# A transformer block in three-term fp32r products: fp32 products put next to each other on TensorE, and two queues reordered in the last rows

## The chip, the core and the metric

The kernel runs on one core of a Trainium2 chip. A core has a matrix engine (TensorE, PE in the profile, whose weight loads are listed as PEld), VectorE (DVE), ScalarE (ACT), GpSimd (POOL) and SyncE (SP), each with an instruction queue of its own that it works off strictly in order, and 16 DMA engines. Matmuls accumulate in PSUM, which here is used as eight banks of 128 x 512 fp32; the other tiles lie in SBUF.

The metric is the time of one execution on the chip, in microseconds (us), as the median of several runs. The profile is taken in an execution of its own, with its own time, and its span is a little shorter than that time.

## The reference, cut to what matters

One transformer block on 512 tokens of 1024 features: a gated linear attention (GLA, 4 heads, keys of 128, values of 256, forward and backward in time), a softmax attention with low-rank queries and keys (MLA, 8 heads, 96 features a head), both merged into one output projection, an MLP with a squared ReLU, and a final norm.

```python
def gla_direction(q, k, v, log_a, include_diag):
    ...
    scores = jnp.where(mask, jnp.einsum('bhnck,bhnsk->bhncs', q_dec, k_dec), 0.0)
    o_intra = jnp.einsum('bhncs,bhnsv->bhncv', scores, v)
    ...
def mla_branch(cq, ckv, kr, positions, g_q, w_uq, g_kv, w_ukv):
    ...
        s = jnp.einsum('bhqd,bhkd->bhqk', qblk, kt).astype(jnp.float32)
        p = jax.nn.softmax(s, axis=-1)
        return jnp.einsum('bhqk,bhkv->bhqv', p.astype(vt.dtype), vt)
    ...
def reference(...):
    h = x
    n = rmsnorm(h, g_mix[l])
    proj = n @ w_in[l]
    ...
    y_gla = gla_branch(...)
    y_mla = mla_branch(...)
    merged = jax.nn.sigmoid(z_ma) * y_gla + jax.nn.sigmoid(z_mb) * y_mla
    h = h + merged @ w_out[l]
    m = rmsnorm(h, g_mlp[l])
    h = h + jnp.square(jax.nn.relu(m @ w_ff1[l])) @ w_ff2[l]
    return rmsnorm(h, g_final)
```

## The kernel before

**Two kinds of products.** Results are wanted to fp32 accuracy. Most products are made of fp32r operands: each operand is split into a high part (an ACT copy to fp32r) and a low part (a DVE subtraction), and `mm3` (line 128) issues three matmuls, high by high, high by low, low by high, into one PSUM bank. Some products have plain fp32 operands instead: the transposes, which are matmuls with an identity matrix (`tp`, `y1`, `kt`, `mb`); the products of blocks `bd` and part of `sc` in the linear attention; and the sums over features by a column of ones (`ckvss`). The profile writes "f32" for both kinds; an fp32 product that is not a transpose stands in it as two records. A transpose is written as one. PSUM tiles come from `ps(tag, name)` (line 118) with two tags, "at" and "mm", of four banks each.

**Stages.** After projections of the input (to about 174 us in the trace), heads 0 to 2 of the linear attention run, each beside gates, projections and norms of the next (loop at `for h in range(GH - 1)`, instructions recorded as line 90). Then comes a stretch from head 3 of the linear attention through the whole softmax attention and the output projection (about 251 to 410 us, recorded as line 76), then the MLP in eight phases (line 90), and the last rows (about 704 us to the end, line 76).

**Orders written out by hand.** For the two stretches recorded as line 76, the class `Held` (line 58) first collects each instruction under its engine and the name of the tile that it writes, and `emit` then issues them in the order of a string, `SEQUENCE` or `LAST_ROWS`. An entry is an engine's letter (P TensorE, A ACT, D DVE, G GpSimd, S SyncE), the tile's name and a count: `P:tp000*4` is four matmuls into tile tp000. Since each engine works in order and waits by semaphores for the others, only the order within one engine counts; how the engines' entries interleave in the string does not. Outside these stretches the order of TensorE, ACT, DVE and GpSimd in the part in question is the program's order.

**Linear attention scores.** For a head, `gla_scores` (line 700) makes, with blocks of 128 tokens j = 0 to 3 of keys: `bd`, four products of the backward direction's diagonal blocks; `sc0` and `sc1`, one bank for two blocks of keys each, with the diagonal block and the neighbouring one; `kt`, four transposes of the keys for the state. From head 1 on, the even blocks of keys (j = 0, 2) are taken as a pair: `split_pairs` has split the keys and queries, and one `mm3` of 256 columns replaces two fp32 products. The odd blocks (j = 1, 3) stay two fp32 products each. Then ACT copies bd to SBUF (`bds`), and DVE's `copy_predicated` writes the part above the diagonal of bds into sc, for j = 0, 1, 2, 3 in turn; ACT rounds sc0 and sc1 to fp32r, DVE makes their low parts, and kt is split into `kT`. Head 0 has no pairs. For head 3 the same instructions stand in SEQUENCE.

Behind gla_scores, for heads 0 to 2, the program goes on with the next head's gates (`gatef` and `gateb`, then logarithms, scans and exponentials on ACT and DVE), a latent projection (`ckv` in head 2), the state, and so on. Head 2 ends with the products `ckv1`, `zb4`; zb4's weights are split on ACT (`zb4h`) and DVE (`zb4l`).

**Softmax attention.** For head h and 128 queries qt, `att_scores` makes a bank `s{h}{qt}` (three matmuls), DVE's maximum (`top`), ACT's exponential (`e`, with its sum `tot`); `att_normalise` scales e. `att_flip(h, half)` transposes two such e: bank `tp{h}{half}{g}`, g = 0, 1, four transposes each, and its split into `pT{h}{x}{g}`, ACT high, DVE low. `att_values` multiplies with the values (`av`). Beside these run the projections of two heads each, `uq`, `uk`, `uv`, and the first products of w_out (`wox`, `woz`, `wow`). `y1` (entries y14, y15) are the transposed outputs of the linear attention, `ckvss` the sums of squares of the latent, whose use DVE continues with `ckvr`.

**Last rows.** The output is finished row block by row block, 0 to 3, in `last_rows` (line 1878). For a block i, `h` is its sum with the MLP's output, `junk` the squares whose sums give the norm (into `hp`), and `ms` the output before it is stored: scaled by the gain and the norm. Row block 3's left half comes in two quarters; its last quarter is accumulated in bank `gend`, with which TensorE ends. `g341l` is the low part of a weight block for the last products.

Of the kernel before, what the change touches and what calls it, by code (L numbers as in the profile page):

```python
# [97 lines left out]
def tile_block(ctx: ExitStack, tc: tile.TileContext, t, out: bass.AP):  # L98
# [1922 lines left out]
    for x in range(2):  # L2021
# [3 lines left out]
        S:w2_11 S:zb6f S:w2_01 S:wr0f*2 A:sin A:zb6h D:cqc2 S:wk0f D:zb6l S:wr0f P:bd*4 D:cqc0 S:wr1f P:sc0*5  # L2025
        A:cqhl0 S:wr1f P:ckvss*4 D:ckvr D:cqc1 P:kt*4 S:wr1f D:ckvr P:y15*4 A:cqhl1 G:ckvr A:bds P:sc1*5 A:cqhl2
        D:sc0 P:y14*4 D:zb4 A:wr0h A:wk0h D:ckvr D:cqhl2 G:wr0l A:wk0h A:qF D:sc1*2 D:cqhl0 A:sc1 S:wk1f D:ckvrh
        D:ckvdg D:krsin D:ckvrl D:ckvdg D:cqhl1 D:sc1 P:zb5*24 A:wr1h D:sc0 A:yg4 D:zb5 G:wr1l A:cos D:kswap A:yg5
        G:wk0l S:wq0f P:ro0*9 A:kT D:kr P:ckvrs*2 S:wq0f A:wk1h A:wk0h G:wk1l S:wq0f A:sc0 D:roa1 G:qF A:wk0h
# [8 lines left out]
        S:q111 P:s11*3 A:yg6 G:wk2l D:tot00 D:e01 S:kbuf3 A:e00 G:wk1l D:top11 A:e03 S:q111 P:uk1*6 D:q101 S:bo11f
        A:kbuf2 P:s02*3 A:wq2h S:q111 A:e11 P:s10*3 G:wq2l S:bo11f D:top10 P:tp000*4 S:w2_20 D:top02 A:e10 A:e02
        P:uv11*12 P:tp001*3 A:wk2h D:tot02 D:kbuf2 A:pT000 G:wk2l D:tot10 A:tb6 S:kbuf3 D:pT010 P:uv10*12 P:tp001  # L2040
        S:w2_00 A:v10 P:s12*3 A:e02 S:q100 D:top12 A:pT001 S:q100 D:e03 A:bo11h S:wk3f D:v10 P:uv00*12 S:q101 A:yg7
        P:s13*3 P:uq2 D:top13 A:v00 S:kbuf2 P:tp010*4 A:e10 D:e11 S:q101 D:pT011 A:e13 D:v00 A:e12 P:uq2*8 D:bo11l
        A:wk2h A:pT000 P:s31*3 G:wk2l A:tb7 P:tp011*4 D:top31 S:wq3f A:wk3h P:tp100*4 P:av0 D:pT010 A:q200 S:wq3f
        A:e31 D:q201 D:tot12 P:uk2*6 D:e13 A:kbuf0 P:tp101*4 S:q301 A:pT001 P:s21*3 S:h3 A:wk2h D:pT011 A:e12
        G:wk2l D:top21 A:pT101 S:bo10f A:pT100 D:pT111 S:bo10f A:e21 P:av0*11 D:pT110 S:wq3f A:wk3h P:tp110*4
        D:kbuf0 A:pT100 P:s20*3 A:v11 D:pT110 S:kbuf1 P:s23*3 S:w2_00 D:top23 P:s22*3 S:q211 D:tb0 A:e23 P:tp111*4
        S:q210 D:top20 G:my0 A:pT101 S:q210 D:top22 A:e20 G:mx0 P:uv20*12 S:w2_10 D:pT111 A:bo10h P:s33*3 D:tot20
        D:top33 A:e22 P:s30*3 D:e21 S:q201 A:e33 P:s32*3 D:top32 S:q200 D:tot22 D:top30 A:e32 S:q200 D:bo10l A:e20
        S:kbuf0 A:e22 S:q201 P:av1*12 D:e23 A:e30 S:bo20f P:tp201*4 A:pT201 D:tot30 P:tp200*4 D:tb1 S:q300 A:pT200
        P:tp210*4 D:pT211 G:mx0 A:wk3h P:s53*3 A:e30 D:tot32 D:pT210 G:my0 A:pT200 D:top53 G:w2_00 D:pT210  # L2050
        P:uv21*12 A:wq3h P:tp211*4 D:e31 A:e53 P:s52*3 P:av2 A:pT201 D:top52 A:gao0 P:s43*3 D:top43 A:e52 G:gao0
        P:s40*3 D:pT211 A:v20 D:top40 A:e43 P:av2*5 G:wk3l D:tot52 D:v11 G:wq3l A:e40 P:tp300*4 D:e33 P:s42*3 A:e32
        G:wk3l S:bo21f A:e52 D:e53 P:s41*3 P:uq3 S:w2_30 G:wk3l P:tp301*4 D:top41 S:q310 A:pT301 D:v20 S:bo21f
        A:e41 P:av2*5 D:top42 S:w2_01 A:v21 S:q311 A:pT300 D:v21 S:w2_21 D:pT310 P:uq3*8 S:w2_11 A:q300 D:tot40
        P:s51*3 P:av2 A:e42 S:q300 D:top51 P:tp310*4 S:q301 D:tb2 A:pT300 S:w2_31 A:e51 D:tot42 D:pT310 P:uk3*6
        S:q311 A:e40 D:e43 S:w2_21 P:s50*3 D:e41 A:q310 G:my1 D:pT311 S:q310 P:tp311*4 A:pT301 P:tp401*4 D:top50
        G:mx1 S:bo20f A:e42 D:pT311 S:w2_31 A:wk3h D:q311 A:kbuf2 G:wk3l A:e50 D:kbuf2 G:yo0 A:pT401 D:tot50
        P:av3*12 D:q301 G:zo1 A:kbuf3 P:tp400*4 D:pT411 G:w2_20 A:pT400 P:tp410*4 A:pT400 P:s61*3 G:w2_11 D:top61
        P:s60*3 G:w2_01 D:top60 A:e61 D:kbuf3 A:e60 P:uv31*12 D:pT410 A:bo50h P:tp411*4 P:av4 D:tb3 A:pT401 P:s62*3
        D:tot60 D:pT410 G:mx1 A:e60 D:top62 G:yo0 D:e51 A:e62 G:my1 P:uv30*12 D:pT411 A:v31 P:s63*3 G:yo1 D:top63  # L2060
        A:e50 P:s71*3 A:ghyo0 D:e61 G:w2_21 D:top71 A:e63 P:av4*4 G:w2_20 D:bo50l A:e71 P:tp510*4 P:tp500*4 A:pT500
        D:tot62 P:s70*3 S:w2_00 A:v30 D:top70 P:tp600*4 S:h2 A:gao1 D:e63 A:pT500 S:h0 D:pT510 G:gao1 A:pT600 S:h1
        D:v30 P:av4*7 D:pT510 G:yo1 P:wox0*3 D:tb4 P:tp501*4 G:zo0 A:pT501 P:wox1*3 G:glyo0 A:e70 D:pT511 P:s72*3
        P:av5 D:pT610 P:tp511*4 G:my2 D:top72 A:pT501 P:s73*3 D:tot70 G:mx2 A:ghyo1 D:pT511 P:av5*2 A:e62 G:zo2
        D:e71 P:tp601*4 A:pT601 G:glyo1 D:v31 A:e72 D:top73 A:e70 P:av5*9 D:pT611 A:e73 P:wox0 P:tp610*4 D:tot72
        A:pT600 D:tb5 P:tp700*4 A:pT700 P:tp701*4 D:pT610 G:my2 P:tp611*4 D:pT710 A:pT601 G:yo2 P:wox1*3 A:e72
        D:pT611 G:mx2 P:woz1*3 A:bo20h P:wox0*2 G:zo0 P:av6 A:bo21h D:bo20l G:yo2 P:av7*5 A:gdo2 A:pT701 D:e73
        A:gao2 G:zo1 D:pT711 A:f010h P:av6*11 G:zo2 D:tb6 P:wow1*3 D:gao2 G:mx3 P:tp710*4 A:pT700 P:wow0*3 A:ghyo2
        D:pT710 G:w2_21 A:gao3 P:av7*7 D:f010l G:w2_10 P:wow1*3 D:gao3 P:wow0*3 G:w2_00 D:bo21l P:tp711*4 A:pT701
        P:wox1*3 A:bo60h D:tb7 D:pT711 P:wox1*3 G:mx3 A:gdo0 D:bo60l P:wox0*3 G:my3 A:ghzo2 A:gao3 A:ghzo1 D:h1  # L2070
        P:av7*12 D:gao3 D:glyo2 P:wox0*3 A:bo31h D:tb7 P:wow1*3 D:h0 G:my3 P:wox1*3 D:bo31l A:gdo2 P:wow0*3
        P:woz1*3 D:yo3*2 P:wow1*3 D:h1 P:wow0*3 D:zo3 A:bo51h D:h0 P:woz0*6 A:ghbo3 D:bo51l A:bo61h P:wox0*3 D:zo3
        P:wox1*3 S:w2_01 A:ms1 D:glbo3 S:w221f P:wox0*3 A:ms0 D:bo61l A:ghzo0 P:woz0*3 A:bo30h G:glzo0 P:woz0*3
        D:h2 P:woz1*3 D:bo30l G:w2_21 P:wox1*3 G:hp0 P:wox1*3 G:glzo1 D:h1 P:wox0*3 D:glzo2 P:woz1*3 G:w2_20
        A:bo71h P:wox0*3 D:h0 A:ghco3 A:bo70h D:glco3 D:h3 D:bo70l P:woz0*12 D:bo71l A:bo41h D:h0 S:w2_11 D:gdo2
        P:woz1*12 A:ms0 S:w2_10 D:h1 S:w2_30 A:gdo0 D:gdo2 A:ms1 S:w220f D:hp0 D:gdo0 G:hp0 A:bo40h S:w2_31 G:hp1
        D:ms0 D:hp1 A:ms0 P:wox0*12 G:hp1 D:h2 A:ms1 D:ms1 A:f011h P:wox1*6 D:bo41l P:mb02 P:mb01 P:mb02 P:mb00
        P:mb01 P:mb00 P:mb02 P:mb00*2 D:gdo0 P:mb03 G:w2_10 A:mr10 D:bo40l A:ms2 A:f050h P:wox1*6 G:hp2 D:f011l
        P:mb03 P:mb02 P:mb01 P:mb03*2 P:mb01 A:mr21 A:mr10 D:h3 A:f020h D:f050l A:mr11 A:mh1 A:mr11 P:wox0*12
        A:mr21 D:h2 A:ms3 D:ml1 A:mr20 G:hp3 A:mh1 G:w2_01 A:mr20 D:ml1 A:mh2 G:w2_00 P:wox1*12 A:ms2 D:ml2 A:mh2  # L2080
        D:h3 A:f021h D:hp2 D:f020l G:hp2 A:ms3 D:hp3 D:ms2 G:hp3 D:ms3 D:ml2 A:f051h D:f021l D:f051l G:w2_01
        G:w2_11
# [132 lines left out]
```

## Time and profile before

| | |
|---|---|
| three runs | 733.16, 733.29, 733.78 us, median 733.29 |
| the profiled execution's own time | 733.74 us |
| its span | 732.0 us |
| mean granted clock of TensorE | 0.999 |
| HBM read, written | 104.22 MB, 2.10 MB; 145 GB/s over the span |
| transposes of e into tp | 128 matmuls, 17.9 us by their records, mean 272 ns |
| ACT's and DVE's halves of the split into pT | 32 each, 18.6 and 21.7 us |
| scores s | 96 matmuls, 26.6 us, mean 403 ns |
| DVE's maxima, ACT's exponentials | 32 each, 21.6 and 21.9 us |

How to read it: the busy time of an engine counts the stretches in which at least one of its instructions runs. Matmuls are pipelined, and the length of a matmul's record reaches from its start to its modelled end, so records overlap and their sum says less than the distance from one start to the next. The clock is the share of full speed that TensorE was granted. In the lists of groups, "idle" is the time in which an engine stood ahead of such an instruction, and behind the arrow stands what ended it.

### The profile page before, as it was taken

Reading aid. Unit: us, or ns where it says so; the run is one execution under the profiler, and the core shown is the slowest. Engines: PE = TensorE matmul, PEld = TensorE weight load, DVE = VectorE, ACT = ScalarE, POOL = GpSimd, SP = SyncE. Lnnn points to the kernel's source line nnn. Section 1 sums busy time; section 2 is a strip of 40 time slices with the busy share of each in tenths; the row PEclk is TensorE's granted clock in tenths of the full one; section 3 lists DMA queues with packets and bytes.
Section 4 is the critical chain, followed back from the end, with each engine's and each line's share of the span. In section 5 each row is a group of like instructions: output and inputs, shape, how many; then the busy total and the mean of one; then the engine's idle time right before and its main releaser. Section 6 shows DMA issues by size and latency. Waiting matters only on the chain.

```text
span 732.0 us, 11458 instructions
## 1 busy us (share of the span) xinstructions
PE 726.9 (99%) x4174; PEld 641.4 (88%) x4174; DVE 621.4 (85%) x861; ACT 502.2 (69%) x853; POOL 224.6 (31%) x283
## 2 busy tenths in 40 slices
...
...
PEclk9999999999999999999999999999999999999999
...
GB/s 303 287 130 197 198 193 94 72 58 45 58 59 59 73 62 96 194 157 187 242 102 194 205 201 203 188 218 54 244 181 205 9 225 202 205 59 138 179 90 142
DMA packets 81625, 109.96 MB, mean 150 GB/s; under 512 B 16256, under 2 KB 35584, under 8 KB 81568
## 3 DMA queue, kind: packets, MB, share of 16 engines
...
q10 hardware_dynamic: 288, 0.22, 0.1%
...
HBM read 104.22 MB, written 2.10 MB: 145 GB/s over the span
## 4 chain that ended last, share of the span: by engine, by line
PE 97%; ACT 1%; POOL 1%; issue 1%; DVE 0%; POOLq 0%; ACTq 0%
PE first L90 3%; PE f3x L90 3%; PE f2x L90 3%; PE f1x L90 3%; PE f0x L90 3%; PE s L76 3%; PE av L76 3%; PE wox L76 3%; PE g2x L90 3%; PE g1x L90 3%; PE g0x L90 3%; PE gvx L90 3%; PE zax L90 3%; PE grx L90 3%; PE gk L90 2%; PE cq L90 2%
## 5 line engine op out<-in xcount | busy, mean ns | idle before, releaser
...
L76 ACT ACTIVATE e<-s,top 128x512 f32<-128x512 f32 x32 | 21.9, 687 | 8.1 <-DVE top L76 7.1
L76 PE MATMUL s<-kbuf,q 96*128 96x512 f32 x96 | 26.6, 403 | 0.0
L76 DVE TENSOR_REDUCE top<-s 128x1 f32<-128x512 f32 x32 | 21.6, 684 | 5.7 <-PE s L76 5.4
L76 PE MATMUL av<-pT,v 128*128 128x512 f32 (+1 forms) x108 | 25.4, 372 | 0.0
L76 DVE TENSOR_TENSOR pT<-tp,pT 128x512 fp32r<-128x512 f32 x32 | 21.7, 685 | 2.2 <-PE s L76 0.9
L76 ACT ACTIVATE pT<-tp 128x512 fp32r<-128x512 f32 x32 | 18.6, 600 | 5.8 <-PE tp L76 5.5
L76 PEld LDWEIGHTS av<-pT,v 128*128 128x128 f32 x108 | 18.6, 189 | 3.3
L76 PEld LDWEIGHTS s<-kbuf,q 96*128 96x128 f32 x96 | 17.0, 189 | 3.1 <-DVE grb L76 0.2
L76 PE MATMUL tp<-ident,e 128*128 128x128 f32 x128 | 17.9, 272 | 0.0
L76 PEld LDWEIGHTS tp<-ident,e 128*128 128x128 f32 x128 | 15.2, 140 | 2.7 <-ACT e L76 0.3
...
L90 POOL TENSOR_TENSOR qF<-qk,qF 128x512 fp32r<-128x512 f32 x3 | 5.3, 1757 | 32.8 <-ACT qF L90 32.8
...
L90 DVE TENSOR_TENSOR w<-w,w 128x1024 f32<-128x1024 f32 x12 | 14.4, 1222 | 0.1
...
L76 POOL TENSOR_TENSOR my<-tb,yg 128x256 f32<-128x256 f32 x8 | 7.2, 899 | 13.7 <-DVE tb L76 7.5
L76 ACT ACTIVATE e<-e,tot 128x512 f32<-128x512 f32 x16 | 11.3, 721 | 0.0
L90 ACT ACTIVATE f1h<-f1a 128x512 fp32r<-128x512 f32 x10 | 6.1, 623 | 6.2 <-DVE f1a L90 6.2
L90 ACT ACTIVATE f0h<-f0a 128x512 fp32r<-128x512 f32 x10 | 6.1, 623 | 6.2 <-DVE f0a L90 6.2
...
## 6 DMA issues: line engine op xcount, KB each, us to landing
...
w221f<-in_w_ff SPq DMA_DIRECT2D x8, 512.0 KB, 5.0
```

The source lines that it names most:

```text
L76: what(*args, **options)
L90: return what(*args, **options)
```

## The change

It leaves the computation and the number of instructions as they are, and changes four orders.

In `gla_scores`, for heads with pairs (1, 2 and 3), the fp32 products of the odd keys stand directly behind `bd`, then the transposes `kt`, and the two fp32r pairs come last. Head 0 is as before.

```diff
-        for j in range(NT):
+        for j in (1, 3) if pairs else range(NT):
             n = j + 1 if j % 2 == 0 else j - 1
-            if pairs and j % 2 == 0:
-                (kh, kl), (qh, ql) = ([t_[:, x, j // 2] for x in range(2)] for t_ in pairs)
-                qh, ql = (q.rearrange("p a b -> p (a b)") for q in (qh, ql))
-                mm3(scs[j // 2][:, 0:256], kh, kl, qh, ql, True, True)
-                continue
             nc.tensor.matmul(block(j, j), near["f"][:, 1, j], near["f"][:, 0, j], start=True, stop=True)
             nc.tensor.matmul(block(j, n), nxt[:, 1, j], nxt[:, 0, n], start=True, stop=True)
         kt = ps("at", "kt")
         for j in range(NT):
             nc.tensor.transpose(kt[:, j * P : (j + 1) * P], far[:, 1, j], ident)
+        for g in range(2) if pairs else ():
+            (kh, kl), (qh, ql) = ([t_[:, x, g] for x in range(2)] for t_ in pairs)
+            qh, ql = (q.rearrange("p a b -> p (a b)") for q in (qh, ql))
+            mm3(scs[g][:, 0:256], kh, kl, qh, ql, True, True)
```

In SEQUENCE TensorE's entries change in six places. Only TensorE's entries of those places are shown here; the strings are wrapped anew as a whole.

```diff
-P:bd*4 P:sc0*5 P:ckvss*4 P:kt*4 P:y15*4 P:sc1*5 P:y14*4 P:zb5*24
+P:bd*4 P:sc0*2 P:sc1*2 P:ckvss*4 P:y15*4 P:y14*4 P:kt*4 P:sc0*3 P:sc1*3 P:zb5*24
...
-P:s10*3 P:tp000*4 P:uv11*12 P:tp001*3 P:uv10*12 P:tp001
+P:s10*3 P:uv11*12 P:tp000*4 P:tp001*4 P:uv10*12
...
-P:s13*3 P:uq2 P:tp010*4 P:uq2*8 P:s31*3 P:tp011*4 P:tp100*4 P:av0 P:uk2*6 P:tp101*4 P:s21*3 P:av0*11 P:tp110*4 P:s20*3
+P:s13*3 P:uq2 P:uq2*8 P:s31*3 P:tp010*4 P:tp011*4 P:tp100*4 P:uk2*6 P:s21*3 P:av0*12 P:tp110*4 P:tp101*4 P:s20*3
...
-P:av2*5 P:tp300*4 P:s42*3 P:s41*3 P:uq3 P:tp301*4 P:av2*5
+P:av2*5 P:s42*3 P:s41*3 P:uq3 P:tp300*4 P:tp301*4 P:av2*5
...
-P:av4*4 P:tp510*4 P:tp500*4 P:s70*3 P:tp600*4
+P:av4*4 P:s70*3 P:tp500*4 P:tp510*4 P:tp600*4
...
-P:wox0*3 P:tp501*4 P:wox1*3 P:s72*3 P:av5 P:tp511*4 P:s73*3
+P:wox0*3 P:wox1*3 P:s72*3 P:av5 P:tp501*4 P:tp511*4 P:s73*3
```

The order of the splits follows. On ACT, `tb7` comes ahead of the first pT000 that reads tp010, pT101 behind the second pT100, and the first pT501 behind the exponential e70. On DVE, pT111 comes behind the second pT110, and the first pT511 behind pT610 and the maximum top72. The orders of GpSimd and SyncE in SEQUENCE stay.

In LAST_ROWS the order of two engines changes. On DVE, `ms1` (row block 1's left half, scaled) moves from behind the first `h3` shown below (row block 3's right half) to ahead of `g341l`, and the second `h3`, the sum of row block 3's first quarter, moves ahead of `hp2`. On ACT, the square of that quarter (a `junk`) moves from behind ms2 to between hp2 and ms2. TensorE, GpSimd and SyncE stay.

```diff
-D:h2 D:hp1 ... D:g341l ... D:ms0 ... D:h3 ... D:ms1 ... D:h2 D:hend ... D:hp2 ... D:h3 ... D:ms2 D:ms3 D:hp3
+D:h2 D:hp1 D:ms1 ... D:g341l ... D:ms0 ... D:h3 ... D:h2 D:hend ... D:h3 D:hp2 ... D:ms2 D:ms3 D:hp3
...
-A:hp2 A:ms2 A:junk A:junk A:hp3
+A:hp2 A:junk A:ms2 A:junk A:hp3
```

More of the change, by code (lines that the diff above doesn't have):

```diff
@@ L2024, in tile_block @@
     SEQUENCE = """
[L2025 to L2029, printed above, removed]
+        S:w2_11 S:zb6f S:w2_01 S:wr0f*2 A:sin A:zb6h D:cqc2 S:wk0f D:zb6l S:wr0f P:bd*4 D:cqc0 S:wr1f P:sc0*2 P:sc1*2
+        A:cqhl0 S:wr1f P:ckvss*4 D:ckvr D:cqc1 P:y15*4 P:y14*4 P:kt*4 S:wr1f D:ckvr P:sc0*3 A:cqhl1 G:ckvr A:bds
+        P:sc1*3 A:cqhl2 D:sc0 D:zb4 A:wr0h A:wk0h D:ckvr D:cqhl2 G:wr0l A:wk0h A:qF D:sc1*2 D:cqhl0 A:sc1 S:wk1f
+        D:ckvrh D:ckvdg D:krsin D:ckvrl D:ckvdg D:cqhl1 D:sc1 P:zb5*24 A:wr1h D:sc0 A:yg4 D:zb5 G:wr1l A:cos D:kswap
+        A:yg5 G:wk0l S:wq0f P:ro0*9 A:kT D:kr P:ckvrs*2 S:wq0f A:wk1h A:wk0h G:wk1l S:wq0f A:sc0 D:roa1 G:qF A:wk0h
         D:roa0 D:kr P:ro1*9 G:wk0l D:ckvc0 D:ckvc1 A:ckvhl0 D:ckvhl0 D:kT A:tb5 D:rob1 A:wk1h D:rob0 A:kbuf0 D:roa0
@@ L2038, in tile_block @@
[L2038 to L2082, printed above, removed]
+        S:q211 A:q000 S:q110 A:kbuf0 S:wq2f P:uv01*12 A:kbuf1 D:kbuf0 S:q110 A:gla3sq A:v01 G:gla3ss S:kbuf2 G:gla3ss
@@ new lines, in tile_block @@
+        A:wq1h S:q011 A:wk1h G:gla3ss A:q010 G:wq1l S:q010 D:grc D:grb S:q010 D:kbuf1 S:wq2f D:q011 S:w2_10 D:q001
+        S:wk2f D:grb D:v01 S:q011 P:zb7*24 D:zb7 S:q211 P:s00*3 D:grc S:q210 P:s01*3 S:w2_20 D:top01 S:w2_30 D:top00
+        S:wq2f A:e00 P:uq1*9 A:tb4 P:y17*4 A:q100 P:y16*4 A:e01 P:s03*3 S:q110 D:top03 A:wk2h S:q111 P:s11*3 A:yg6
+        G:wk2l D:tot00 D:e01 S:kbuf3 A:e00 G:wk1l D:top11 A:e03 S:q111 P:uk1*6 D:q101 S:bo11f A:kbuf2 P:s02*3 A:wq2h
+        S:q111 A:e11 P:s10*3 G:wq2l S:bo11f D:top10 S:w2_20 D:top02 A:e10 A:e02 P:uv11*12 P:tp000*4 P:tp001*4 A:wk2h
@@ new lines, in tile_block @@
+        D:tot02 D:kbuf2 A:pT000 G:wk2l D:tot10 A:tb6 S:kbuf3 D:pT010 P:uv10*12 S:w2_00 A:v10 P:s12*3 A:e02 S:q100
+        D:top12 A:pT001 S:q100 D:e03 A:bo11h S:wk3f D:v10 P:uv00*12 S:q101 A:yg7 P:s13*3 P:uq2 D:top13 A:v00 S:kbuf2
+        A:e10 D:e11 S:q101 D:pT011 A:e13 D:v00 A:e12 P:uq2*8 D:bo11l A:wk2h P:s31*3 G:wk2l A:tb7 P:tp010*4 P:tp011*4
+        A:pT000 D:top31 S:wq3f A:wk3h P:tp100*4 D:pT010 A:q200 S:wq3f A:e31 D:q201 D:tot12 P:uk2*6 D:e13 A:kbuf0
+        S:q301 A:pT001 P:s21*3 S:h3 A:wk2h D:pT011 A:e12 G:wk2l D:top21 S:bo10f A:pT100 S:bo10f A:e21 P:av0*12 D:pT110
@@ new lines, in tile_block @@
+        S:wq3f A:wk3h P:tp110*4 P:tp101*4 D:kbuf0 A:pT100 P:s20*3 A:pT101 A:v11 D:pT110 S:kbuf1 P:s23*3 S:w2_00
+        D:pT111 D:top23 P:s22*3 S:q211 D:tb0 A:e23 P:tp111*4 S:q210 D:top20 G:my0 A:pT101 S:q210 D:top22 A:e20 G:mx0
+        P:uv20*12 S:w2_10 D:pT111 A:bo10h P:s33*3 D:tot20 D:top33 A:e22 P:s30*3 D:e21 S:q201 A:e33 P:s32*3 D:top32
+        S:q200 D:tot22 D:top30 A:e32 S:q200 D:bo10l A:e20 S:kbuf0 A:e22 S:q201 P:av1*12 D:e23 A:e30 S:bo20f P:tp201*4
+        A:pT201 D:tot30 P:tp200*4 D:tb1 S:q300 A:pT200 P:tp210*4 D:pT211 G:mx0 A:wk3h P:s53*3 A:e30 D:tot32 D:pT210
@@ new lines, in tile_block @@
+        D:top63 A:e50 P:s71*3 A:ghyo0 D:e61 G:w2_21 D:top71 A:e63 P:av4*4 G:w2_20 D:bo50l A:e71 P:s70*3 P:tp500*4
+        A:pT500 D:tot62 P:tp510*4 S:w2_00 A:v30 D:top70 P:tp600*4 S:h2 A:gao1 D:e63 A:pT500 S:h0 D:pT510 G:gao1
+        A:pT600 S:h1 D:v30 P:av4*7 D:pT510 G:yo1 P:wox0*3 D:tb4 G:zo0 P:wox1*3 G:glyo0 A:e70 P:s72*3 P:av5 D:pT610
+        P:tp501*4 P:tp511*4 A:pT501 G:my2 D:top72 D:pT511 A:pT501 P:s73*3 D:tot70 G:mx2 A:ghyo1 D:pT511 P:av5*2 A:e62
+        G:zo2 D:e71 P:tp601*4 A:pT601 G:glyo1 D:v31 A:e72 D:top73 A:e70 P:av5*9 D:pT611 A:e73 P:wox0 P:tp610*4 D:tot72
@@ new lines, in tile_block @@
+        P:wox0*3 A:bo31h D:tb7 P:wow1*3 D:h0 G:my3 P:wox1*3 D:bo31l A:gdo2 P:wow0*3 P:woz1*3 D:yo3*2 P:wow1*3 D:h1
+        P:wow0*3 D:zo3 A:bo51h D:h0 P:woz0*6 A:ghbo3 D:bo51l A:bo61h P:wox0*3 D:zo3 P:wox1*3 S:w2_01 A:ms1 D:glbo3
+        S:w221f P:wox0*3 A:ms0 D:bo61l A:ghzo0 P:woz0*3 A:bo30h G:glzo0 P:woz0*3 D:h2 P:woz1*3 D:bo30l G:w2_21
+        P:wox1*3 G:hp0 P:wox1*3 G:glzo1 D:h1 P:wox0*3 D:glzo2 P:woz1*3 G:w2_20 A:bo71h P:wox0*3 D:h0 A:ghco3 A:bo70h
+        D:glco3 D:h3 D:bo70l P:woz0*12 D:bo71l A:bo41h D:h0 S:w2_11 D:gdo2 P:woz1*12 A:ms0 S:w2_10 D:h1 S:w2_30 A:gdo0
@@ new lines, in tile_block @@
+        D:gdo2 A:ms1 S:w220f D:hp0 D:gdo0 G:hp0 A:bo40h S:w2_31 G:hp1 D:ms0 D:hp1 A:ms0 P:wox0*12 G:hp1 D:h2 A:ms1
+        D:ms1 A:f011h P:wox1*6 D:bo41l P:mb02 P:mb01 P:mb02 P:mb00 P:mb01 P:mb00 P:mb02 P:mb00*2 D:gdo0 P:mb03 G:w2_10
+        A:mr10 D:bo40l A:ms2 A:f050h P:wox1*6 G:hp2 D:f011l P:mb03 P:mb02 P:mb01 P:mb03*2 P:mb01 A:mr21 A:mr10 D:h3
+        A:f020h D:f050l A:mr11 A:mh1 A:mr11 P:wox0*12 A:mr21 D:h2 A:ms3 D:ml1 A:mr20 G:hp3 A:mh1 G:w2_01 A:mr20 D:ml1
+        A:mh2 G:w2_00 P:wox1*12 A:ms2 D:ml2 A:mh2 D:h3 A:f021h D:hp2 D:f020l G:hp2 A:ms3 D:hp3 D:ms2 G:hp3 D:ms3 D:ml2
```

36 lines of the change are left out of this document (24 added, 12 removed).

## The prediction

> **What bounds the kernel now.** I read the page first, then the busy time by stages, then the chain in order of time.
>
> ```profile
> span 732.0 us, 11458 instructions
> PE 726.9 (99%) x4174; PEld 641.4 (88%) x4174; DVE 621.4 (85%) x861; ACT 502.2 (69%) x853; POOL 224.6 (31%) x283
> PEclk9999999999999999999999999999999999999999
> 290.00:384.00 94.00, 94.00 (x533) 80.58 (x531) 81.77 (x144) 76.00 (x164) 47.14 (x52) 1.00 0.73 176
> ```
>
> TensorE is busy for 99% of the span and for all 94 us of the attention stage (the columns there are stage, length, PE, PEld, DVE, ACT, POOL, clock). Its clock is full. So an edit counts in two ways only: by the TensorE time that an order of the same products takes, and by waits that the new order puts into TensorE. The exception is the end, from 726 us on, where TensorE has finished and ACT and DVE close the span. Since ends of matmuls are modelled, I measure by distances between starts.
>
> The profiled execution took 733.74 us with a span of 732.0; the median of the three runs is 733.29. I add my sum to the median; against the profiled execution's own time the result would be 0.45 us higher.
>
> **What one run of fp32 products costs.** "fp32" here are transposes and products whose operands are both fp32; all the others are fp32r.
>
> ```profile
> 174.52 0.89 PE bd L90 x8
> 175.41 1.79 PE sc L90 x16
> 279.05 2.07 PE uq L76 x9
> 305.86 0.40 PE L76 MATMUL uq<-cqhl,wq2h 128*128 128x512 f32 x1
> 306.09 0.60 PE L76 MATMUL tp<-ident,e 128*128 128x128 f32 x4
> 306.45 0.48 PE L76 MATMUL uq<-cqhl,wq2h 128*128 128x512 f32 x1
> 308.38 0.40 PE L76 MATMUL s<-kbuf,q 96*128 96x512 f32 x1
> 363.87 1.91 PE L76 MATMUL tp<-ident,e 128*128 128x128 f32 x16
> 365.53 0.48 PE L76 MATMUL wox<-bo10h,gao 128*128 128x512 f32 x1
> ```
>
> The first three rows are of the chain (start, length); an fp32 product stands as two records, so bd's 8 and sc's 16 are 4 and 8 products, at 0.111 us a record. The run of 16 transposes takes 1.66 us up to the next start, the last one being followed early: 15 at 0.109 and one at about 0.03. So a run of four takes 0.36 instead of 0.44, and the next fp32r product in turn takes longer. Is that worth a merge? uq is interrupted once: 308.38 - 305.86 = 2.52 us for nine products and four transposes. Uninterrupted, nine take 2.07, and four transposes inside a longer run 0.44: 2.51. A run thus costs **about 0.01 to 0.02 us**, not more. What a boundary could cost at most is the length of a transpose's record (0.60 for four means 0.27 for one) less its step of 0.109, about 0.16 us, as if the array ran empty; the uq row lies near zero, and I take 0.015.
>
> **The probabilities' transposes.** In SEQUENCE their runs fall by seven: tp000 with both parts of tp001; tp010, tp011 and tp100 in one, tp110 and tp101 in one (four runs to two); tp300 with tp301; tp500, tp510, tp600; tp501 with tp511. No instruction is added.
>
> ```profile
> 308.54 0.70 PE s L76 x3
> 308.84 0.62 ACT L76 ACTIVATE pT<-tp 128x512 fp32r<-128x512 f32 x1
> 309.32 0.66 ACT L76 ACTIVATE tb<-zb 128x512 f32<-128x512 f32 x1
> ```
>
> 7 x 0.015 = **-0.1 us** (ends: 0 and 7 x 0.16 = -1.1). Do waits arise? The latest mover is tp010: it started at 306.09 and now follows uq2 and s31, at 305.86 + 2.07 + 0.70 = 308.63. Its last transpose ends at 308.63 + 3 x 0.109 + 0.27 = 309.23, and its split on ACT, which stood at 308.84, waits for that; tb7 (the 0.66), put ahead of it, fills the time. tp501 comes 1.6 us later, behind seven products, and its split then runs behind e70; tp511 ends where it did. s70 comes 0.8 us earlier, into a bank that came free longer ago, since the pool hands out the oldest. I find no place where the new need comes before the bank or the operand, by margins of 0.1 to 0.9 us, and put the waits at nothing (upper end under the rivals).
>
> **The scores of the linear attention, heads 1 and 2.** In `gla_scores` odd keys (fp32) and key transposes now come first, the fp32r pairs last.
>
> ```profile
> 227.43 1.05 PE L90 MATMUL bd<-qkb 128*128 128x128 f32 x8
> 228.24 0.60 PE L90 MATMUL sc<-qk,qk 128*128 128x256 f32 x3
> 229.04 0.60 PE L90 MATMUL sc<-qk,qk 128*128 128x256 f32 x3
> 229.93 0.60 PE L90 MATMUL kt<-ident,qk 128*128 128x128 f32 x4
> 230.28 0.48 PE L90 MATMUL gatef<-z,gate_f 128*128 128x512 f32 x1
> 230.83 0.63 PE L90 MATMUL ckv<-xT,ckv0h 128*128 128x512 f32 x2
> 202.44 1.15 DVE L90 COPY_PREDICATED sc<-after,bds 128x128 f32<-128x128 int32 x4
> 229.39 1.37 DVE L90 COPY_PREDICATED sc<-after,bds 128x128 f32<-128x128 int32 x4 [1.07 <-PE sc L90]
> 230.12 1.34 ACT L90 ACTIVATE sc<-sc 128x512 fp32r<-128x512 f32 x2 [1.00 <-PE sc L90]
> 246.77 1.09 ACT L90 ACTIVATE zb4h<-zb4f 128x1024 fp32r<-128x1024 f32 x1
> 247.89 1.23 DVE L90 TENSOR_TENSOR zb4l<-zb4f,zb4h 128x1024 fp32r<-128x1024 f32 x1 [1.88 <-ACT zb4h L90]
> 249.29 0.40 PE L90 MATMUL zb<-xT,zb4l 128*128 128x512 f32 x1
> ```
>
> TensorE gains nothing: from bd to ckv it takes 230.83 - 227.43 = 3.40 us; the new order is bd 0.89 + sc 0.89 + kt 0.36 + pairs 0.44 + 0.36 + gates 0.47 = 3.41.
>
> But sc0, its pair first, was complete at 229.04; now its pair comes last and ends at 227.43 + 0.89 + 0.89 + 0.36 + 0.44 = 230.01. DVE's first masked copy needs exactly that block and starts 0.24 to 0.35 after it, at 230.25, not 229.39. It stood waiting for TensorE already (the 1.07 in brackets), so nothing hides this. The third copy no longer waits for sc1, which gives back a little: four copies without a wait took 1.15 in head 1, so they end at 231.40 instead of 230.76, 0.64 later. Between 0.64 and the first copy's 0.86 I take 0.7, and by that much later come ACT's two copies of sc, the key split, the gates' logarithms, scans and exponentials, which follow each other on ACT and DVE in a fixed order. That order ends, for TensorE, at zb4l: done at 249.12, used at 249.29. Part of the wait shows already at ckv1's first product, whose bank the same queue frees. The spare 0.17 is used up, and TensorE loses 0.7 - 0.17 = **+0.53 us** (ends: 0, if idle time in between takes the delay; 0.86 - 0.17 = 0.69, if nothing is given back). In head 1 the copies stood behind DVE's own queue, not behind TensorE; they come only 0.5 later, and what follows on TensorE there has over 1 us to spare: nothing.
>
> **Head 3, in SEQUENCE.** Three fp32 runs become one, at the same sum as above.
>
> ```profile
> 256.00 0.95 PE L76 MATMUL ckvss<-ones,ckvs 128*128 128x1 f32 x8
> 256.99 0.16 DVE L76 SCALAR_TENSOR_TENSOR ckvr<-ckvss,r_x 128x4 f32<-128x4 f32 x1 [0.72 <-PE ckvss L76]
> 264.58 0.69 DVE L76 TENSOR_TENSOR cqhl<-cqc,cqhl 128x512 fp32r<-128x512 f32 x1
> 265.12 0.69 PE L76 MATMUL ro<-cqhl,wr0h 128*128 128x512 f32 x2
> ```
>
> ckvss now follows two bd/sc blocks without the short last step: 254.31 + 0.89 + 0.89 = 256.09, 0.09 later. DVE waits for it, and its queue runs on to cqhl, which ends at 265.27; the two ro products beside it span 0.69 where ckv's two above span 0.63, so TensorE waits for it already. **+0.09 us** (ends 0 and 0.15). sc0 and sc1 are ready by 258.8 and 259.2, before DVE gets to them; kt, y14 and y15 find their operands long finished.
>
> **Last rows.** DVE's ms1 moves ahead of g341l, h3 ahead of hp2; on ACT the square of row 3's first quarter moves ahead of ms2.
>
> ```profile
> 719.80 1.23 DVE L76 TENSOR_TENSOR g341l<-w,g341h 128x1024 fp32r<-128x1024 f32 x1 [0.41 <-ACT g341h L76]
> 722.20 1.46 DVE L76 SCALAR_TENSOR_TENSOR ms<-h,hp,gfin 128x512 f32<-128x512 f32 x1
> 723.58 0.68 DVE L76 TENSOR_TENSOR h<-h,g3x 128x512 f32<-128x512 f32 x1
> 725.58 0.41 DVE L76 TENSOR_TENSOR h<-g3x,h 128x256 f32<-128x256 f32 x1
> 725.76 0.72 ACT L76 ACTIVATE ms<-ms,hp 128x512 f32<-128x512 f32 x1 [0.29 <-DVE hp L76]
> 726.39 0.40 ACT L76 ACTIVATE junk<-h 128x256 f32<-128x256 f32 x1
> 726.79 0.36 ACT L76 ACTIVATE junk<-gend 128x256 f32<-128x256 f32 x1
> 726.17 0.28 PE L76 MATMUL gend<-g341h,f3l 128*128 128x256 f32 x1
> ```
>
> The span ends behind the square of gend, at 726.79. gend itself is complete at 726.17 + 0.28 = 726.45; ACT is late by 0.3. With ms1 gone from 722.20, h2 starts 0.18 earlier, at 723.4, and all behind it; the quarter's square fills ACT's 0.29 ahead of ms2. The square of gend then waits for TensorE alone, at 726.50: **-0.28 us** (ends 0 and -0.3). What it costs: ms1 starts in DVE's idle 0.41 ahead of g341l and delays its end, 721.03, by its own length less that, 0.3 (if it takes 0.7, as the other such rows without POOL beside them) to 1.05 (if 1.46); the first product with g341l stands about 1.0 us after that end. I take the cost as nothing (up to 0.1).
>
> **Sum**: -0.1 + 0.53 + 0.09 - 0.28 = +0.24: 733.29 + 0.24 = **733.5 us**, which is +0.03%. About 0.2% (1.5 us) is what a measurement of this kernel can tell from no change.
>
> **Rivals.**
> 1. The delay in head 2 is taken up on the way. For it: ACT has gaps before zb4h; against it: the gaps that I find end with the very chain that is late. Then -0.1 - 0.28: 732.9.
> 2. Boundaries cost what the record lengths allow, 0.16 each. 13 runs fall away (7, and 2 in each of three heads): -2.1, 731.4. Against it speaks uq's 2.52. The Trainium skill (TensorEngine Tiling, Key Properties) says that a change of tiling mode drains the array; no run here shows a drain at a change of operand type, and if the rule reached that far the sum would be this one.
> 3. Slower: flips that come later hold up ACT, whose queue is in order. The point is where a split waits longer than what is put ahead of it, as at tp010 (0.4 against tb7's 0.6). If four places passed on one split each, 0.6 us: 4 x 0.6 = 2.4, 735.9. A milder form, 0.8 in all, gives 734.3. Against it: the lanes there have time left (ACT 76 of 94 us).
> 4. Slower: long fp32 stretches lower the clock. In head 3 one lasts 0.89 + 0.89 + 0.82 + 0.87 + 0.36 = 3.8 us (bd, sc, ckvss, y, kt); at half clock it would cost as much again: 737.3. Against it: 16 transposes in one run of 1.66 us stand in the trace at full clock. The Trainium skill (TensorE: Matmul & The Clock Gate, Part 4: PE-mode transpose) says that transposes do not count as activity for the clock gate; by the trace's full clock at 363.87 us such a run is too short for it, and the new one has 12 transposes.
>
> **Chances.** Forecast 0.52, rival 1 0.22, mild rival 3 0.14, rival 2 0.05, full rival 3 0.05, rival 4 0.02. The range takes in the forecast, rival 1 and the mild rival 3 with 0.3 us around them: 732.5 to 734.6. Faster by over 0.2% 0.05, within 0.2% 0.88, slower 0.07.
>
> **What would show it.** In the new profile: the copies of sc in head 2 begin about 0.86 us later after bd than now; a longer step at ckv1's and zb4's first products; seven fewer runs of tp in the stage of attention, with the same length within 0.2 us; the square of gend right behind its last product. A step of TensorE that shortens by more than 0.1 at a merge, zb4l in time, or a wait behind a flip would make me wrong.

## The result, and the profile after

The changed kernel takes **738.03 us** (median of six runs, 737.05 to 739.75); the kernel before takes 733.46 (six runs, 733.16 to 735.14). The ratio is 1.0063, with a 95% interval of 1.0052 to 1.0073: 4.6 us slower. The forecast was 733.5, in a range from 732.5 to 734.6.

The profiled execution is the longest of the six, 739.75 us with a span of 738.0. Two lines of its page, and below them one row of its busy time by stages, with the columns of the row that the prediction shows of before:

```profile
span 738.0 us, 11456 instructions
...
PE 93%; ACT 2%; DVE 2%; DMA 2%; issue 1%; SPq 0%; DVEq 0%; ACTq 0%
```

```profile
290.00:390.00 100.00, 96.72 (x534) 82.33 (x533) 82.00 (x145) 75.89 (x164) 46.94 (x52) 0.98 0.70 166
```

The attention stage, 94 us with TensorE never idle before, takes 100 us for the same work, and TensorE stands idle in 3.3 of them, at a mean clock of 0.98. The chain of work that ended last, 97% TensorE before, now leaves it for a load. These are its pieces from there on, in order of time (start, length, what):

```profile
315.33 0.67 PE tp L76 x6
316.00 0.02 SPq L76
...
317.28 0.38 SPq L76
317.66 0.05 issue
317.72 6.89 DMA bo10f<-in_w_out
...
324.71 0.04 ACT bo10h L76
324.75 0.92 issue
325.68 0.77 ACT e L76 x2
...
328.44 2.82 PE tp L76 x12
```

Read it from the end. Twelve transposes (tp200, tp201, tp210) wait for exponentials; those stand on ACT behind `bo10h`, the high half of a w_out block; bo10h waits for the load of bo10f; the load was issued late, by a queue that was let go at 316.00 by transposes of the probabilities. SyncE's instructions show that queue, before and after (start, length of the issue):

```profile
309.55 0.90 SPq L76 DMA_DIRECT2D wq3f<-in_w_uq  x2
312.02 0.51 SPq L76 DMA_DIRECT2D q<-ro  x1
...
314.00 0.82 SPq L76 DMA_DIRECT2D bo10f<-in_w_out  x2
```

```profile
309.93 0.90 SPq L76 DMA_DIRECT2D wq3f<-in_w_uq  x2
316.05 0.51 SPq L76 DMA_DIRECT2D q<-ro  x1
316.62 0.57 SPq L76 DMA_DIRECT2D h<-in_x  x1
317.28 0.86 SPq L76 DMA_DIRECT2D bo10f<-in_w_out  x2
```

And from the list of waits of SyncE after (total, times, longest; before, the same line says 1.5):

```profile
SPq L76 <- PE tp L76: 5.2, 1, 5.2
```

The load in question is `q301`, a part of the queries of head 3. What can it have to do with transposes of head 1? The SBUF tiles of the tag "u2" take turns in 29 buffers (`u2`, line 109): q301 gets the buffer of the probabilities `e10`, and may write there only when `tp100` and `tp101` have read them. The change moves tp101 from 311.57 us, between uk2 and s21, behind av0 and tp110. After, tp110 and tp101 are one run of eight from 315.17 (TensorE's instructions, with the wait ahead of one and its end in brackets):

```profile
315.17 1.03 PE L76 MATMUL tp<-ident,e 128*128 128x128 f32 x8
317.07 2.48 PE L76 MATMUL s<-kbuf,q 96*128 96x512 f32 x9 [0.87 <-ACT e L76]
```

At steps of 0.109 us the sixth, the last of tp101 that reads e10, begins at 315.17 + 5 x 0.109 = 315.71 and with a length of 0.27 ends at 315.99. SyncE goes on at 316.05. The eighth, the last that reads e11, ends at 316.20, and ACT shows who waited for that one:

```profile
316.24 0.69 ACT L76 ACTIVATE e<-s,top 128x512 f32<-128x512 f32 x1 [1.83 <-PE tp L76]
...
324.71 1.06 ACT L76 ACTIVATE bo10h<-bo10f 128x1024 fp32r<-128x1024 f32 x1 [2.91 <-DMA bo10f<-in_w_out]
```

`e21` writes into the buffer of e11. In the trace of before, ACT already waited a little for that load, and the twelve transposes behind it did not wait:

```profile
320.59 1.06 ACT L76 ACTIVATE bo10h<-bo10f 128x1024 fp32r<-128x1024 f32 x1 [0.60 <-DMA bo10f<-in_w_out]
...
324.42 1.47 PE L76 MATMUL tp<-ident,e 128*128 128x128 f32 x12
```

So the load had no time to spare. In two other traces whose order there is that of before (x4_heads_alone and x7_tail_alone, below) TensorE itself waits 0.35 and 0.64 us at these transposes, ACT 1.19 and 1.49 us for the load.

Behind the wait comes a second loss. The busy time by stages after, in two stretches: the wait, and what follows (the last three columns are granted clock, DMA share, GB/s):

```profile
325.69:328.44 2.75, 0.59 (x4) 0.17 (x2) 1.97 (x4) 2.75 (x9) 0.00 (x0) 0.99 0.58 123
328.44:332.10 3.66, 3.66 (x16) 3.47 (x17) 2.38 (x6) 3.41 (x8) 1.57 (x3) 0.54 0.33 69
```

Over the 3.66 us behind the wait TensorE has a mean clock of 0.54: it is 0.50 from 328.39 to 331.80 us and 1.00 behind that. The twelve transposes take 2.82 us here, by steps of 0.213 and not 0.109.

A third place lies at tp501, which the change moves behind s72 (ACT and TensorE, after):

```profile
364.74 1.04 PE L76 MATMUL tp<-ident,e 128*128 128x128 f32 x8
...
365.20 0.69 ACT L76 ACTIVATE e<-s,top 128x512 f32<-128x512 f32 x1 [2.48 <-issue]
...
366.03 0.96 PE L76 MATMUL s<-kbuf,q 96*128 96x512 f32 x3 [0.26 <-ACT e L76]
```

`e70` stands 2.48 us on ACT, and s73 waits for it on TensorE. The view names no releaser for that wait. By the program, e70 takes the buffer of e50, and the last to read e50 is the second transpose of tp501, which ends at 364.74 + 0.109 + 0.27 = 365.12, just ahead of e70's start.

How far TensorE's starts lie behind those of before, in the profiled execution and in a second one of the changed kernel (`x11_after_again` below, 737.85 us, span 736.1):

| TensorE at | before, us | second profile | profile after |
|---|---|---|---|
| gates of head 2 | 230.28 | -0.22 | -0.32 |
| zb5, behind head 3's scores | 258.89 | +0.53 | +0.41 |
| av beside uq3 | 334.17 | +3.85 | +5.68 |
| av4, behind tp500 | 355.10 | +3.81 | +5.63 |
| s73 | 359.90 | +4.31 | +6.13 |
| last product of gend | 726.17 | +4.37 | +6.20 |
| end of the span | 732.0 | +4.1 | +6.0 |

So the parts are: +0.74 at the heads' scores, +3.3 (with half clock +5.3) from there to the av beside uq3, the stretch with tp101, nothing at the merges behind it, +0.5 at tp501, 0.2 to 0.3 gained at the end.

### The profile page after: what moved, and what is told of

The parts are those of the page before. It is cut to its first block, busy times and chain, and to the rows that moved or that the text cites. A ratio compares the mean times of both kernels' runs of the same rounds, so it can differ in the third digit from the quotient of the medians.

```text
span 738.0 us, 11456 instructions
## 1 busy us (share of the span) xinstructions
PE 729.4 (99%) x4174; PEld 641.8 (87%) x4174; DVE 621.2 (84%) x861; ACT 501.6 (68%) x853; POOL 222.7 (30%) x283
## 4 chain that ended last, share of the span: by engine, by line
PE 93%; ACT 2%; DVE 2%; DMA 2%; issue 1%; SPq 0%; DVEq 0%; ACTq 0%
PE f2x L90 3%; PE f3x L90 3%; PE f1x L90 3%; PE f0x L90 3%; PE g0x L90 3%; PE g2x L90 3%; PE g1x L90 3%; PE gvx L90 3%; PE zax L90 3%; PE grx L90 3%; PE wox L76 3%; PE av L76 2%; PE s L76 2%; PE gk L90 2%; PE gq L90 2%; PE zb L76 2%
## 5 line engine op out<-in xcount | busy, mean ns | idle before, releaser
L90 ACT ACTIVATE f2h<-f2a 128x512 fp32r<-128x512 f32 x10 | 6.1, 621 | 6.2 <-DVE f2a L90 6.2
```

Source lines behind the costliest of these rows:

```text
L90: return what(*args, **options)
```

## The experiments

All are compared with runs of the kernel before on the same chip, whose medians were 733.50 (first four), 733.40 (next four), 733.32 (x9, x10) and 732.83 (one run, x11, x12).

**One mover put back.** `x1_tp101_back`, against the changed kernel:

```diff
-P:uk2*6 P:s21*3 P:av0*12 P:tp110*4 P:tp101*4 P:s20*3
+P:uk2*6 P:tp101*4 P:s21*3 P:av0*12 P:tp110*4 P:s20*3
-A:pT100 A:e21 ... A:pT100 A:pT101
+A:pT101 A:pT100 A:e21 ... A:pT100
```

(and pT111 on DVE back ahead of the second pT110).

> The changed kernel with one mover put back: tp101's four transposes again between uk2 and s21, and with them their splits (pT101 on ACT, pT111 on DVE). Theory 'buffer': the loss in the attention stage comes from SBUF buffers that tp101 frees by reading the probabilities e10 and e11; SyncE's load into q301 waits for the one and ACT's e21 for the other. Then the wait on SyncE falls from 5.2 us to about 1.5, ACT no longer waits 2.9 us for the load of bo10f, the step from -0.2 to +5.3 us between 311 and 337 us shrinks to within 0.3, and the time comes to about 734.0 us (0.6 for the heads, 0.5 at e70, 0.3 less at the end): 733.6 to 734.8. Rival 'long fp32 runs': it is the length of the runs of fp32 products or the mere order on TensorE that costs; one run more would give back under 0.3 us, and the time stays above 737.

Measured: 734.37 us, ratio 1.0014 (1.0004 to 1.0023). Of the 4.6 us, 3.7 are gone with four transposes moved back. SyncE's wait for tp is down from 5.2 us to 1.3 (1.5 before), and ACT's wait for bo10f is gone. "Long fp32 runs" falls.

**That mover alone.** `x2_tp101_alone` is the same edit the other way, in the kernel before.

> The kernel before with this one mover alone: tp101's transposes behind av0 and tp110, their splits pT101 and pT111 behind those of the second pT100 and pT110. Theory 'buffer': the whole loss of the attention stage stands here too, 3.5 to 5.5 us: 737 to 739, with a wait of about 5 us on SyncE for tp and 2 to 3 us on ACT for the load of bo10f. Rival 'many small waits': the loss is the sum of several movers, and this one alone gives under 2 us: below 735.3.

Measured: 737.19, ratio 1.0060 (1.0040 to 1.0081): +3.7 (2.9 to 5.9), the same amount from the other side. SyncE waits 5.3 us for tp, ACT 2.2 us for the load of bo10f. In the profiled execution (736.23 us, the shortest of the four) TensorE then waits 1.46 us at the twelve transposes, with full clock behind it. The sum of many small waits falls too.

**SyncE's wait without its followers.** `x3_q301_later`, against the changed kernel:

```diff
-S:q301 S:h3 S:bo10f S:bo10f S:wq3f S:kbuf1
+S:h3 S:bo10f S:bo10f S:wq3f S:q301 S:kbuf1
```

> The changed kernel with SyncE's load of q301 issued four entries later, behind the loads of h3, bo10f (2) and wq3f; TensorE, ACT and DVE as in the changed kernel. It tells the two waits for tp101 apart. Theory 'SyncE': the load of q301 holds up the load of bo10f behind it in the queue, and ACT stands on bo10h; then bo10f is issued at about 314 us as before, ACT's wait for it is below 1 us, and the time falls to 734.5 to 736 (what is left is e21's wait on ACT, 1.8 us of which 1.5 reached TensorE, the heads and e70). Theory 'ACT': e21's wait for tp101 on ACT alone starts the delay and the load only comes on top of it; then the time stays above 737.

Measured: 735.87, ratio 1.0034 (1.0021 to 1.0047). bo10f is issued at 314.68, and ACT goes from an exponential to bo10h at 322.01 with no wait. What stays is e21:

```profile
316.55 0.69 ACT L76 ACTIVATE e<-s,top 128x512 f32<-128x512 f32 x1 [1.61 <-PE tp L76]
...
322.01 1.05 ACT L76 ACTIVATE bo10h<-bo10f 128x1024 fp32r<-128x1024 f32 x1
```

Against x1_tp101_back, where neither wait stands, that is 735.87 - 734.37 = 1.5 us for e21's wait (1.3 by the distance from zb5 to the av behind tp500 in the two traces, 97.43 against 96.17), and 738.03 - 735.87 = 2.2 for the load's on top of it.

**The loads alone, twice.** In the kernel before, `x8_bo10f_later` delays only bo10f, `x10_group_later` the whole group, both behind kbuf1, which waits for DVE until about 316 us. No other queue is touched.

```diff
-S:q301 S:h3 S:bo10f S:bo10f S:wq3f S:kbuf1
+S:q301 S:h3 S:wq3f S:kbuf1 S:bo10f*2
...
+S:kbuf1 S:q301 S:h3 S:bo10f*2 S:wq3f
```

> The kernel before with SyncE's order alone changed: the two loads of bo10f go behind wq3f and kbuf1 and so are issued at about 317.1 us instead of 314.0; TensorE, ACT, DVE and POOL as before. It measures by itself what the late load costs, which in the changed kernel was issued at 317.3. Theory 'SyncE': ACT waits 2.5 to 3 us longer ahead of bo10h, the exponentials behind it come later, and TensorE loses 2 to 3.5 us at tp200, tp201: 735.5 to 737. Rival: TensorE has other work there, and the loss needs e21's wait as well: below 734.5.

Measured: 734.11, ratio 1.0009 (1.0000 to 1.0019): +0.7 (0.0 to 1.4), a miss. bo10f was issued 2.4 us later by the clock of the trace, at 316.43, and 3.2 later counted from the same product on TensorE, and yet bo10h started at 320.46. The load landed sooner, as the DMA issues show (KB each, median us from issue to landing; before, after, x8):

```profile
bo10f<-in_w_out SPq DMA_DIRECT2D x2, 256.0 KB, 5.5
```

```profile
bo10f<-in_w_out SPq DMA_DIRECT2D x2, 256.0 KB, 6.3
```

```profile
bo10f<-in_w_out SPq DMA_DIRECT2D x2, 256.0 KB, 3.3
```

Behind h3's 512 KB the same load took 5.5 and 6.3 us here, and 3.3 once h3 had landed; the expectations of x9 and x10 below took h3 for the cause. Other traces speak against that. In six of them h3 is issued 1.42 us ahead of bo10f, and the load takes 5.5, 6.3 and 6.5 us in three (before, x4, x7), but 3.8, 4.1 and 3.7 in the others (x1, x5, x6). In the slow three kbuf1 follows 2.56 us behind bo10f's issue, in the fast three 2.80; no run changes that alone, and what sets the landing time stays open. The next experiment delays the whole group.

> The kernel before with SyncE's order alone changed: the load kbuf1, which waits for DVE until about 316.5 us, stands ahead of q301, h3, bo10f (2) and wq3f, so that the whole group starts at about 317 us, nearly as it does in the changed kernel (316.1); TensorE, ACT, DVE and POOL as before. It measures the late group by itself, without e21's wait. Theory 'burst': bo10f lands at about 325 us, ACT waits 4 to 6 us ahead of bo10h, and TensorE loses 3.5 to 6 us at tp200 and tp201: 737 to 739.5; if TensorE then stands idle for over 2 us, its granted clock falls to half in the slice behind, as in the changed kernel (0.50 from 328.4 to 331.0). Rival: without e21's wait the loss is below 2 us: under 735.4.

Measured: 738.28, ratio 1.0073 (1.0058 to 1.0088): +5.0 without e21's wait and with TensorE's order as before. ACT, TensorE, and the stretch behind:

```profile
322.93 1.06 ACT L76 ACTIVATE bo10h<-bo10f 128x1024 fp32r<-128x1024 f32 x1 [3.30 <-DMA bo10f<-in_w_out]
```

```profile
326.66 2.82 PE L76 MATMUL tp<-ident,e 128*128 128x128 f32 x12 [2.45 <-ACT e L76]
```

```profile
326.66:330.30 3.64, 3.64 (x15) 3.47 (x16) 2.38 (x6) 3.38 (x8) 1.55 (x3) 0.54 0.43 103
```

A wait of 2.45 us, and half clock behind it, as in the changed kernel. ACT's wait was 3.3 us, less than the 4 to 6 expected, and bo10f itself took 4.4 us, less than the 5.5 of before. Counted from zb5's first product it was issued 4.1 us later than before, in x8 3.2. So bo10h started 2.7 us later than before here and 0.6 later in x8, and the kernel lost 5.0 us here and 0.7 there: in this pair the loss follows the start of the consumer.

**Another order of the group.** `x9_h3_later`, in the changed kernel: h3 behind bo10f and wq3f, all still behind q301.

```diff
-S:q301 S:h3 S:bo10f S:bo10f S:wq3f S:kbuf1
+S:q301 S:bo10f S:bo10f S:wq3f S:h3 S:kbuf1
```

> The changed kernel with SyncE's load of h3 (512 KB) put behind those of bo10f and wq3f; q301 still waits for tp101 ahead of them all. In x8_bo10f_later the two loads of bo10f came 3 us later and yet landed in 3.3 us instead of 5.5, because h3 was no longer in flight beside them. Theory 'burst': in the changed kernel h3 and bo10f start together after the wait, and it is their sum that lands late; with h3 behind, bo10f is issued at 316.6 and lands 3.3 to 4.5 us later, ACT waits under 0.7 us ahead of bo10h, and what is left is e21's wait: 735.4 to 736.4, as in x3_q301_later. Rival: bo10f lands no earlier, since the loads that follow share the engines as well: the time stays above 737.

Measured: 742.44, ratio 1.0127 (1.0110 to 1.0144); the profiled execution took 737.74, the others 742.2 to 744.4. bo10f now lands in 4.2 us, as expected, and ACT's wait for it falls from 2.9 to 1.1, not below the 0.7 expected. But the time went up by another 4.4 us and not down. kbuf1, now behind h3, takes 8.2 us in this profile, but it took 7.7 in the changed kernel's, so that is not the reason. A second profile, `x12_h3_later_again`, was to show it:

> The kernel of x9_h3_later once more, for a second profile: the profiled execution there took 737.74 us, the four others 742.2 to 744.4. Theory 'clock': in an execution of over 742 us TensorE waits for the loads that follow bo10f (kbuf, the rotated parts of q) for over 2 us in a place where it waited 0.6 us in the profile at hand, and runs at half clock behind it. Rival: a single further wait of 5 us with full clock behind it.

Measured: 744.12. TensorE's scores s and the busy time of the stretch that begins with them:

```profile
336.19 3.08 PE L76 MATMUL s<-kbuf,q 96*128 96x512 f32 x6 [3.24 <-DMA kbuf<-kbuf]
```

```profile
336.18:340.00 3.82, 3.81 (x9) 2.71 (x10) 1.98 (x5) 0.78 (x2) 1.45 (x3) 0.50 0.57 179
```

TensorE waits 3.24 us for kbuf, and half clock follows: the part of the theory about the clock holds. The delay had only been handed to another load of the queue: this is kbuf's second transfer, issued at 330.51, behind a copy of q parts that took 7.58 us, and landed 5.54 us later. In x9's profile, the one execution of the six that took 737.74 us, TensorE waited 0.24 us for the same transfer. Why it came soon enough there stays open.

**The spread.** `x11_after_again` is the changed kernel, profiled a second time.

> The changed kernel once more, for a second profile: its six runs lay between 737.05 and 739.75 us, and the profile is that of 739.75. Theory 'clock': after TensorE's wait of 2.3 us at tp200 the granted clock is 0.5 for about 3.6 us in that execution, which costs 1.65 us of the difference, and an execution near 737 us has a shorter wait there and no slice at half clock. If this execution takes under 737.8, its steps of tp behind the wait are 0.109 us and not 0.213; if it takes over 739, they are 0.213 again. Rival: the spread has nothing to do with the clock there; then the steps don't go with the time.

Measured: 737.85 us, just above the 737.8 that the expectation names, with the steps of 0.109 us that it expects below that. The same transposes and the same stretch as above:

```profile
328.18 1.53 PE L76 MATMUL tp<-ident,e 128*128 128x128 f32 x12 [1.78 <-ACT e L76]
```

```profile
328.44:332.10 3.66, 3.66 (x32) 3.52 (x30) 2.71 (x8) 3.43 (x9) 1.84 (x3) 1.00 0.34 72
```

The wait is 1.78 us and not 2.15, and the clock behind it stays full. By the table above the two executions part at this place, by 1.83 us (+3.85 against +5.68), and of their difference of 1.9 nearly all is that, 0.4 as the longer wait and the rest as half clock. The Trainium skill (TensorE: Matmul & The Clock Gate, Why this matters for your kernels) sets the limit for an idle gap at about 3 us; here 2.15 and 2.45 us were enough and 1.78 was not. Nor were 1.46 (x2) and 1.52 us (x12, ahead of the other wait). In these traces half clock lasts 3.41 us (328.39 to 331.80 after, 326.61 to 330.02 in x10) or twice that (335.60 to 342.43 in x12, where it begins 0.59 us before the wait of 3.24 us ends). Whether the length of a wait alone decides is not shown: in the three runs the waits also differ in where they lie in time.

**The other parts.** `x4_heads_alone` has only the new order of the scores, in the kernel before; `x5_tp501_back` is x1_tp101_back with the second mover put back:

```diff
-P:wox0*3 P:wox1*3 P:s72*3 P:av5 P:tp501*4 P:tp511*4
+P:wox0*3 P:tp501*4 P:wox1*3 P:s72*3 P:av5 P:tp511*4
```

> The kernel before with the new order of the scores in heads 1, 2 and 3 alone (the fp32 products of odd keys first, key transposes, pairs last; in the head of the handwritten sequence with the two y blocks as the change has them). Theory: the later sc0 in head 2 makes zb4l late, +0.53 us, and ckvss in head 3 costs 0.09: 733.9 to 734.1 against a before of 733.3, and zb4's first low product comes 0.5 to 0.6 us later after bd. Rival: the delay is taken up by idle time, and the time stays within 0.2 us of before.

Measured: 734.43, ratio 1.0013 (1.0004 to 1.0023): +0.9 (interval +0.3 to +1.7), and by the trace, zb4's first low product stands 249.66 - 227.16 = 22.50 us behind bd, against 249.29 - 227.43 = 21.86 before, 0.64 later. Its weight load names whom it waits for:

```profile
249.65 0.19 PEld L90 LDWEIGHTS zb<-xT,zb4l 128*128 128x128 f32 x1 [0.48 <-DVE zb4l L90]
```

> The kernel of x1_tp101_back with a second mover put back: tp501 again between wox0 and wox1, its split ahead of the exponential e70, DVE's pT511 ahead of pT610. Theory 'buffer': e70 writes into the buffer that tp501 frees by reading e50; ACT stood 2.5 us for it and s73 behind it on TensorE lost 0.5 us. That goes: the time falls by 0.5 against x1_tp101_back, to 733.9, and ACT waits for no tp ahead of e70. Rival: the 0.5 us belongs to the longer run of transposes or to the early s70; then the time stays at 734.4.

Measured: 734.02, ratio 1.0008 (0.9999 to 1.0017): 0.35 below x1_tp101_back, or 0.25 when each is set against its own runs of before, which is within the noise. The traces show it clearly: by TensorE's starts the step at s73 is gone, 0.5 us (from the av behind tp500 to s73 5.30 us in x1, 4.82 here, 4.80 before). ACT's wait ahead of e70 is gone with it.

`x6_merges_tail` is what is left: five runs of transposes fewer, and the last rows; `x7_tail_alone` the last rows by themselves.

> The kernel before with what is left of the change when the heads' scores, tp101 and tp501 stay as they were: five runs of transposes fewer (tp000 with tp001, tp010 with tp011 and tp100, tp300 with tp301, tp500 and tp510 with tp600), and the last rows in the new order. Theory: a run of fp32 products less is worth 0.01 to 0.02 us (0.05 to 0.1 in all), the last rows 0.3: 0.35 us below before, 733.1 if before is 733.5. Rival 'boundaries': each run is worth 0.16 us, 0.8 in all: 732.4. Rival 'small waits': the merges cost what the last rows give: 733.5.

> The kernel before with the new order of the last rows alone. Theory: the square of gend follows its last product within 0.05 us instead of 0.34, and the time falls by 0.3 us, to 733.2 if before is 733.5. Rival: ms1 ahead of g341l or h3 ahead of hp2 makes a product or the third row block late, and nothing is gained.

Measured: 733.32, ratio 0.9998 (0.9989 to 1.0007), and 733.30, ratio 0.9997 (0.9988 to 1.0005). Neither can be told from no change by the times. The traces give more. The chain's pieces from zb5 to the av behind tp500, before and in x6_merges_tail:

```profile
259.13 2.98 PE zb L76 x13
```

```profile
355.35 1.61 PE av L76 x7
```

```profile
258.98 3.21 PE zb L76 x14
```

```profile
355.14 1.62 PE av L76 x7
```

96.22 us against 96.16: by this pair five runs fewer are worth 0.06 us, 0.012 each. This is a difference of two single executions, not a firm value. By starts, x1 and x5, with the same five merges there, take 96.17, but x4 and x7, with the order of before there, 96.83 and 97.11, since TensorE waits in them behind the load of bo10f. What it does exclude is 0.16 a run: that would be 0.8.

## Why the prediction was wrong

**The merges' waits: this step failed.** "I find no place where the new need comes before the bank or the operand, by margins of 0.1 to 0.9 us, and put the waits at nothing." That was looked up for PSUM banks and operands, thus for what a moved transpose needs. What others need of it was left out: reading e is what frees e's SBUF buffer, and the next tile in the ring of 29 may belong to another engine. "The latest mover is tp010" was wrong as well. tp010 moves by 2.9 us (306.09 to 309.02), tp101 by 4.0 (311.57 to 315.61, the fifth of the eight). At tp101 it cost 3.7 us by x1 and x2 (e21's wait 1.5, the load's 2.2 by x3), at tp501 0.5 by the traces (0.25 to 0.35 by the times). The note that "tp501 comes 1.6 us later" named the mover, and only its split was followed; e70, in the buffer that it frees, lost 2.48 us on ACT.

**Each queue that a step is moved past.** SyncE does not change its order, and the prediction says nothing of it in this stage. But a queue with the old order waits for the new place of a step. Rival 3 had the form, an in-order queue held up by a later flip, with splits on ACT as the waiting part and 0.6 us a place. The real one is a load in SyncE's queue, and its price comes from what stands behind it: bo10f, on ACT bo10h that needs it, and the exponentials behind bo10h.

**The worth of a boundary.** Right in size: 0.015 us a run was forecast, and one pair of traces gives 0.012. Rival 2, 0.16 a run, falls with it.

**Head 2 and 3.** Right in mechanism, low in size: from head 2's bd to head 3's the starts take 27.62 us after and 26.88 before, 0.74 more where 0.53 was forecast. zb4l was done 0.76 later behind bd, not 0.7; only 0.12 of it was taken up, not the 0.17 that was called spare; and the first low product, once waited for, was followed 0.10 later. From head 3's bd to zb6 it is 0.06 more (14.88 against 14.82), where 0.09 was forecast. The first masked copy began 229.87 - 227.03 = 2.84 us behind bd, against 229.39 - 227.43 = 1.96, that is 0.88 later where 0.86 was forecast:

```profile
227.03 1.05 PE L90 MATMUL bd<-qkb 128*128 128x128 f32 x8
...
229.87 1.17 DVE L90 COPY_PREDICATED sc<-after,bds 128x128 f32<-128x128 int32 x4 [1.71 <-PE sc L90]
```

Rival 1, that idle time takes the delay, falls.

**The last rows.** Right: the square of gend was forecast behind its last product with 0.28 gained.

```profile
732.37 0.28 PE L76 MATMUL gend<-g341h,f3l 128*128 128x256 f32 x1
...
732.69 0.38 ACT L76 ACTIVATE junk<-gend 128x256 f32<-128x256 f32 x1
```

It starts 0.04 behind 732.37 + 0.28, where it was 0.34 behind before: 0.30 gained. x7_tail_alone's interval holds that gain and holds none.

**The clock.** Rival 4, long fp32 stretches that lower it, falls: the stretch of head 3 has full clock (254.60 to 259.30, 1.00). Half clock came behind waits of TensorE, a case that the prediction did not have, since it saw no idle time at all.
